# Layer 1's pooling mixer: the projection and the group maps folded into one matrix, token tiles, and pooling as products with integers

## The chip, the core and the metric

The kernel runs on one core of one Trainium2 chip. The metric is the device time of one execution in microseconds (us). TensorE (PE) multiplies, PEld loads its weights, VectorE (DVE) and ScalarE (ACT) work on tiles, GpSimd (POOL) does small tile work and indirect DMAs, SyncE (SP) issues most weight loads. The instruction streams of the engines are fixed when the program is built: each engine takes its instructions in order, and an instruction waits for the tiles that it reads.

## The reference, cut to what matters

1024 tokens of 1024 channels pass two layers. Layer 0 mixes by attention beside an mLSTM, layer 1 by pooling, and each ends in a mixture of 16 experts, each of which chooses its 128 tokens:

```python
def pool_mixer(h, w_in, w_grp, s_pool):
    u = h @ w_in
    S = cumsum(u) padded with one zero row
    for gi, w in enumerate((2, 4, 8, 16)):          # 256 channels each
        lo = w // 2; hi = w - 1 - lo
        a = clip(t - lo, 0, n - 1); e = clip(t + hi, 0, n - 1)
        outs.append((S[e + 1] - S[a]) / (e - a + 1) - u_group)
    y = einsum('bngc,gce->bnge', p, w_grp)
    return y * s_pool

x = x + m2 * pool_mixer(modulate(x, g_norm1, m0, m1), ...)
h = modulate(x, g_norm2, m3, m4)
x = x + m5 * ec_moe(h, w_router, w_gate, w_up, w_down)
```

`modulate` is an RMS norm, times (1 + scale), plus a shift. Pooling acts on tokens alone and the group map on channels alone, so the two can change places.

## The kernel before, in words

Products that need fp32 accuracy are made of three fast ones: `split` writes a high part with an ACT cast (L57) and the rest with a DVE subtraction (L58), and `mm3` (L51 to L53) multiplies high by high, low by high, and high by low.

Layer 0 ends in `out0`: per tile of 128 tokens the output projection `y` (512 wide), the new stream x, `half` (transposes L883, ACT copies L886, squares L888), `logits` (L894, 16 wide, plain fp32), `norm2`, `router`, and `normed`, which stores the normed tokens to G. Then comes `topk`, in which each expert finds its 128 tokens: 15 rounds, each three DVE comparisons (L978), one tiny PE product (L983) and a few DVE instructions on it, then two scans, a transpose (L1016) and a cast (L1018). After that `moe`: `choose` builds an expert's list with a one-hot of DVE (L1174) and eight products (L1178), `gather` fetches its rows with an indirect DMA of POOL (L1166), and the expert is three products of 1024x1024, g, u and d. SP streams the weights in 1 MB pieces through a ring of 17 slots (`cyc`). The last expert's rows go into the stream by products with one-hot matrices (`rows`, L1271 to L1279), so that no indirect DMA stands at the end.

Layer 1 works channel by channel. `w_normed` multiplies a group of `w_in_odd` (256 columns, 1 MB) by the scale (L1343) and sums it with the shift on POOL (L1340 to L1344); for the first group in the last expert of layer 0, for the other three in `layer1`. `turn` (L1292) transposes the stream tile by tile. `channels(i)` makes u of one group with 96 products of 512 columns (channels on the partitions, tokens along the row), and DVE walks along the tokens: times the rows' norms (L1434), doubling window sums (L1440), mean minus token (L1444), the edges (L1448, L1449), and the split. `mapped` multiplies by the group map, 256 wide, for `into_stream` (L1464), which runs for group i - 1 after the products of group i; `done_half` puts half of the logits between the products of the last group. The last group ends tile by tile (L1497) with the norm, the router and the store of the normed tokens. `topk` and `moe` of layer 1 follow, then the final norm.

In `topk` the code sets the order; between its instructions a list scheduler, at build time, places what is ready of the code around it. Which instructions of the changed code stand there is shown below.

Of the kernel before, what the change touches and what calls it, by code (L numbers as in the profile page):

```python
# [11 lines left out]
F32 = mybir.dt.float32  # L12
# [10 lines left out]
D = 1024  # L23
N = 1024
NCTX = 256
NT = 8
# [6 lines left out]
ORDER = (3, 2, 1, 0)  # L33
# [8 lines left out]
class Kern:  # L42
# [996 lines left out]
    def out0(self):  # L1039

        tc, nc, I = self.tc, self.nc, self.I
        with ExitStack() as es:
# [26 lines left out]
            xs = [resid(0), resid(1)]  # L1069
            self.norm2_load(0, (row("r_a2"), row("r_s2")), c.tile([128, KB + 1, 16], F32, name="wr"),  # L1070
# [37 lines left out]
            self.topk(tp, [(psl, "pl")])  # L1108


    def moe(self, l, last=False):
        tc, nc, I = self.tc, self.nc, self.I
        with ExitStack() as es:
# [93 lines left out]
            for e in range(16):  # L1207
# [21 lines left out]
                if e == 15 and not last:  # L1229
                    T = lambda nm, shape: self.topp.tile(shape, F32, name=nm)  # L1230
                    self.al, self.ones = T("al1", [128, 8]), T("ones1", [128, 1])
                    nc.gpsimd.memset(self.ones, 1.0)
# [5 lines left out]
                if e == 15 and not last:  # L1238
                    wn = self.w_normed(w0, self.R(9, (128, KB, 256), F32), xr3.tile([128, 4, 256], F32, name="X3"), nc.vector)
                if e == 15:  # L1240

                    xs, xp = [], []
                    for q, slot in enumerate(self.cyc[l][5:9]):
# [42 lines left out]
            if not last:  # L1286
                self.ss1 = self.topp.tile([128, NT], F32, name="ss1")
                self.xs, self.xp, self.W = xs, xp, [[self.quarters(wn[0])]]
                self.HH = [[self.R(i, (128, 4, 512)) for i in q] for q in ((6, 7), ("X1", "X2"))]
                self.HL = [[self.R(i, (128, 4, 512)) for i in q] for q in ((8, "X0"), (1, 2))]  # L1290

                def turn(t):  # L1292
                    b, os_ = t // 4, slice((t % 4) * 128, (t % 4 + 1) * 128)
                    for c in range(2):
                        ps = pst.tile([128, 4, 128], F32, name="tr", tag="tr")
                        for j in range(4):
                            nc.tensor.transpose(ps[:, j], xs[t][:, (4 * c + j) * 128:(4 * c + j + 1) * 128], self.idf)
                        self.turned = self.split(self.HH[b][c][:, :, os_], self.HL[b][c][:, :, os_], ps)

                for t in range(NT + 1):  # L1300
                    if t < NT:
                        rows(t)
                    if t:
                        turn(t - 1)
                for t in range(NT):
                    square(xs[t], self.ss1[:, t:t + 1])
                self.W[0].append(self.w_shift(wn[1]))
                return
# [19 lines left out]
    def w_raw(self, i):  # L1328

        raw, g = self.R(5, (128, KB, 256), F32), ORDER[i]  # L1330
        self.nc.sync.dma_start(raw, self.I["w_in_odd"][0].rearrange("(k p) n -> p k n", p=128)[:, :, g * 256:(g + 1) * 256])
        return raw

    def w_normed(self, raw, out, t, engine):

        G = self.nc.gpsimd
        acc, tmp = t[:, 0:2], t[:, 2:4]
        for q in range(4):
            b = slice(2 * q, 2 * q + 2)
            G.tensor_tensor(tmp if q else acc, raw[:, b], self.mcol[:, 0, b, None].to_broadcast([128, 2, 256]), op=ALU.mult)  # L1340
            if q:
                G.tensor_tensor(acc, acc, tmp, op=ALU.add)
        engine.tensor_tensor(out, raw, self.al[:, :, None].to_broadcast([128, KB, 256]), op=ALU.mult)  # L1343
        G.tensor_tensor(acc[:, 0], acc[:, 0], acc[:, 1], op=ALU.add)  # L1344
        return out, acc[:, 0]

    def w_shift(self, s1):

        sh = self.topp.tile([128, 2], F32, name="sh1", tag="sh1", bufs=2)
        ps = self.pst.tile([128, 512], F32, name="tr", tag="tr")  # L1350
        for m in range(2):
            self.nc.tensor.matmul(ps[:, m:m + 1], s1[:, m * 128:(m + 1) * 128], self.ones, start=True, stop=True)
        self.nc.vector.tensor_copy(sh, ps[:, 0:2])
        return sh

    def layer1(self):
        tc, nc, I = self.tc, self.nc, self.I
        LO = [w // 2 for w in (2, 4, 8, 16)]
        with ExitStack() as es:
            P = lambda name, bufs=1, **k: es.enter_context(tc.tile_pool(name=name, bufs=bufs, reuse_waits="tile", **k))  # L1360
            gp, hf, sp, c, pst = P("g1", 2), P("hf1", 2), P("st1", 2), P("c1"), self.pst
            up = tc.alloc_tile_pool(name="u1", bufs=1, reuse_waits="tile")
            psu, psy, psl = P("psu1", 2, space=PSUM), P("psy1", 1, space=PSUM), P("psl1", 1, space=PSUM)
            HH, HL, W, xs = self.HH, self.HL, self.W, self.xs

            rc = c.tile([128, 4, 16], F32, name="rc")
            for g, lo in enumerate(LO):
                for t in range(lo):
                    nc.gpsimd.memset(rc[:, g, t:t + 1], 1.0 / (t + lo))
                for t in range(lo - 1):  # L1370
                    nc.gpsimd.memset(rc[:, g, 8 + t:9 + t], 1.0 / (2 * lo - 1 - t))
            r8 = self.rstd(c, self.ss1, D, "r8", True)

            def more_w(i):
                t = self.R(10 if i == 1 else 0, (128, 4, 256), F32)
                raw = self.w_raw(i)
                raw, s1 = self.w_normed(raw, raw, t, nc.gpsimd)
                W.append((self.quarters(raw), s1))

            more_w(1)  # L1380

            ms = c.tile([128, 1024], F32, name="ms")
            with tc.issue_after(self.turned):
                nc.scalar.dma_start(ms, bc(self.MOD[8]))
                sr = up.tile([128, 1024], F32, name="sr", tag="pf")
                nc.scalar.dma_start(sr, bc(I["s_pool"][0]))
                nc.vector.tensor_tensor(ms, ms, sr, op=ALU.mult)

            def invariants():

                R = up.tile([128, 1024], F32, name="R1")
                for q in range(2):
                    ps = pst.tile([128, 512], F32, name="tr", tag="tr")
                    for t in range(4):
                        nc.tensor.matmul(ps[:, t * 128:(t + 1) * 128], r8[:, 4 * q + t:4 * q + t + 1].to_broadcast([128, 128]),
                                         self.idf, start=True, stop=True)
                    nc.scalar.copy(R[:, q * 512:(q + 1) * 512], ps)
                return R

            def channels(i, between=iter(())):  # L1400

                g, lo = ORDER[i], LO[ORDER[i]]
                w = 2 * lo
                cs = slice(g * 256, (g + 1) * 256)
                rg = hf.tile([128, 2, 256], F32, name="rg", tag="hf")
                nc.scalar.dma_start(rg, I["w_pool_grp"][0, g].rearrange("(k p) n -> p k n", p=128))
                nc.vector.tensor_tensor(rg, rg, ms[:, None, cs].to_broadcast([128, 2, 256]), op=ALU.mult)
                gh = gp.tile([128, 2, 256], F32R, name="gh", tag="gh")
                gl = gp.tile([128, 2, 256], F32R, name="gl", tag="gl")
                self.split(gh, gl, rg)  # L1410
                sh = self.w_shift(W[i][1]) if i else W[0][1]
                pu = [psu.tile([128, 1024], F32, name="u", tag="u") for m in range(2)]
                for q in range(2):
                    for m in range(2):
                        for k in range(KB):
                            a = slice(m * 128, (m + 1) * 128)
                            wh, wl = W[i][0][k // 4]
                            self.mm3(pu[m][:, q * 512:(q + 1) * 512], wh[:, k % 4, a], wl[:, k % 4, a], HH[q][k // 4][:, k % 4],
                                     HL[q][k // 4][:, k % 4], k == 0, k == KB - 1)
                        next(between, None)  # L1420
                if i == 0:
                    self.R1 = invariants()
                if i < 3:
# [53 lines left out]
            for i in range(1, 4):  # L1477
                if i + 1 < 4:
                    more_w(i + 1)
# [131 lines left out]
```

## Time and profile before

| | |
|---|---|
| median of 3 runs | 2328.53 us (2322.75 to 2331.19) |
| profiled execution | 2325.28 us, of which the span of the profile is 2323.5 us |
| TensorE busy | 2133.2 us (92%) |
| VectorE busy | 1974.5 us (85%) |
| ScalarE, GpSimd busy | 1407.9 us (61%), 258.1 us (11%) |
| mean granted clock of TensorE | 0.959 |

The span is that of one profiled execution. A share near 100% means that the engine works nearly all the time, but the shares are means over stages with different limits: layer 0 up to about 850 us, its choice up to 889 us, its experts up to about 1481 us, layer 1's mixer and choice up to about 1712 us, and its experts to the end.

### The profile page before, as it was taken

The page shows a single profiled execution, that of the slowest core. Times are in us where ns is not written, and L with a number is a line of the kernel's source. Part 1 is how long each engine was busy: PE and PEld are TensorE (multiplying, and loading weights), DVE is VectorE, ACT ScalarE, POOL GpSimd, SP SyncE. Part 2 cuts the span into 40 slices and gives each one's busy share as a digit, 9 for nine tenths or more (in the row PEclk, how much of TensorE's full clock was granted, in tenths as well). Part 3 has the DMA queues.
Part 4 walks back from the last instruction along what each step waited for, and adds up shares of the span by engine and source line. Part 5 has one row for each costly group of instructions (what it writes and reads, how often), then busy time and mean ns, then how long its engine had stood idle before and what let it go on. Part 6 is the DMA issues. An engine that isn't in the chain of part 4 may idle for free.

```text
span 2323.5 us, 29647 instructions
## 1 busy us (share of the span) xinstructions
PE 2133.2 (92%) x10339; PEld 1702.9 (73%) x10339; DVE 1974.5 (85%) x3043; ACT 1407.9 (61%) x1994; POOL 258.1 (11%) x369
## 2 busy tenths in 40 slices
PE   6889999998988966999999999889749999999997
PEld 3768887776666854888888887568637888888875
DVE  7888755999997558999999998885789999999986
ACT  6412224777784224777777777622337777777774
POOL 0111110000000010000000010550300000000001
PEclk9989999999999987999999999999769999999999
DMA  7566653243325466999999995323859999999974
GB/s 275 201 234 231 244 197 111 75 115 99 90 83 182 163 259 244 365 380 388 385 378 392 380 379 204 111 63 118 326 193 355 387 386 381 388 384 379 391 247 154
DMA packets 206634, 599.39 MB, mean 258 GB/s; under 512 B 16708, under 2 KB 60180, under 8 KB 205460
## 3 DMA queue, kind: packets, MB, share of 16 engines
q1 hardware_dynamic: 168480, 481.81, 55.0%
q0 software_dynamic: 20704, 74.49, 11.1%
q10 hardware_dynamic: 17300, 41.20, 4.8%
q8 instruction: 81, 1.33, 0.2%
q14 instruction: 69, 0.57, 0.1%
HBM read 544.87 MB, written 52.58 MB: 257 GB/s over the span
## 4 chain that ended last, share of the span: by engine, by line
PE 56%; DVE 8%; issue 2%; ACT 2%; POOL 1%; DMA 1%; ACTq 0%; POOLq 0%; DVEq 0%; SPq 0%
PE u L51 6%; PE u L52 6%; PE u L53 6%; PE g L53 5%; PE g L52 5%; PE g L51 5%; PE d L52 5%; PE d L53 5%; PE d L51 5%; PE tr L1158 2%; DVE wl L58 2%; PE y L51 2%; PE y L53 2%; PE y L52 1%; DVE tjunk L978 1%
## 5 line engine op out<-in xcount | busy, mean ns | idle before, releaser
L58 DVE TENSOR_TENSOR wl<-R,wh 128x1024 fp32r<-128x1024 f32 x512 | 614.5, 1236 | 39.0 <-ACT wh L57 36.5
L57 ACT CAST wh<-R 128x1024 fp32r<-128x1024 f32 x512 | 534.1, 1052 | 172.9 <-PE d L53 56.6
L58 DVE TENSOR_TENSOR wl<-X,wh 128x1024 fp32r<-128x1024 f32 x178 | 211.0, 1220 | 13.9 <-ACT wh L57 13.1
L57 ACT CAST wh<-X 128x1024 fp32r<-128x1024 f32 x178 | 186.0, 1050 | 54.8 <-PE d L53 23.2
L52 PE MATMUL d<-wl,ah 128*128 128x512 f32 x512 | 203.6, 398 | 5.5 <-DVE wl L58 5.5
L51 PE MATMUL d<-wh,ah 128*128 128x512 f32 x512 | 205.2, 401 | 2.9 <-DVE o L1193 2.9
L51 PE MATMUL g<-wh,xh 128*128 128x512 f32 x512 | 205.8, 402 | 1.5 <-ACT xh L57 1.5
L52 PE MATMUL g<-wl,xh 128*128 128x512 f32 x512 | 203.2, 397 | 1.8 <-DVE wl L58 1.8
L51 PE MATMUL u<-wh,xh 128*128 128x512 f32 x512 | 204.4, 399 | 0.0
L52 PE MATMUL u<-wl,xh 128*128 128x512 f32 x512 | 202.6, 396 | 0.6 <-DVE wl L58 0.6
L53 PE MATMUL g<-wh,xl 128*128 128x512 f32 x512 | 203.2, 397 | 0.0
L53 PE MATMUL d<-wh,al 128*128 128x512 f32 x512 | 202.7, 396 | 0.0
L53 PE MATMUL u<-wh,xl 128*128 128x512 f32 x512 | 202.1, 395 | 0.0
L57 ACT CAST wh<-raw 128x1024 fp32r<-128x1024 f32 (+1 forms) x112 | 115.5, 1037 | 57.1 <-PE pp L53 15.3
L58 DVE TENSOR_TENSOR wl<-raw,wh 128x1024 fp32r<-128x1024 f32 (+1 forms) x112 | 131.6, 1202 | 13.1 <-ACT wh L57 12.3
L693 ACT ACTIVATE e<-se 128x512 f32<-128x512 f32 x160 | 93.4, 596 | 42.9 <-PE se L691 30.5
L52 PEld LDWEIGHTS d<-wl,ah 128*128 128x128 f32 x512 | 96.9, 189 | 30.2 <-DVE wl L58 9.3
L51 PEld LDWEIGHTS d<-wh,ah 128*128 128x128 f32 x512 | 96.8, 189 | 25.1 <-ACT ah L57 3.8
L51 PEld LDWEIGHTS g<-wh,xh 128*128 128x128 f32 x512 | 97.2, 190 | 23.7 <-ACT xh L57 2.5
L52 PEld LDWEIGHTS g<-wl,xh 128*128 128x128 f32 x512 | 97.1, 190 | 23.7 <-DVE wl L58 2.6
L52 PEld LDWEIGHTS u<-wl,xh 128*128 128x128 f32 x512 | 96.4, 188 | 23.2 <-DVE wl L58 1.9
L53 PEld LDWEIGHTS d<-wh,al 128*128 128x128 f32 x512 | 96.8, 189 | 22.6 <-DVE al L58 0.5
(561 smaller groups left out, 4833.1 us busy)
## 6 DMA issues: line engine op xcount, KB each, us to landing
R<-in_w_exp_gate SPq DMA_DIRECT2D x87, 1024.0 KB
R<-in_w_exp_down SPq DMA_DIRECT2D x85, 1024.0 KB
R<-in_w_exp_up SPq DMA_DIRECT2D x79, 1024.0 KB
wm<-in_w_mod POOLq DMA_DIRECT2D x80, 512.0 KB, 5.2
X<-in_w_exp_up SPq DMA_DIRECT2D x33, 1024.0 KB
X<-in_w_exp_down SPq DMA_DIRECT2D x30, 1024.0 KB
X<-in_w_exp_gate SPq DMA_DIRECT2D x26, 1024.0 KB
raw<-in_w_exp_up SPq DMA_DIRECT2D x16, 1024.0 KB
```

Source lines behind the costliest of these rows:

```text
L51: mm(ps, lh, rh, start=start, stop=False)
L52: mm(ps, lh, rl, start=False, stop=False)
L53: self.mark = mm(ps, ll, rh, start=False, stop=stop).ins
L57: self.nc.scalar.copy(hi, src)
L58: return self.nc.vector.tensor_tensor(lo, src, hi.bitcast(F32), op=ALU.subtract).ins
L693: nc.scalar.activation(e, ps, AF.Exp)
L978: V.tensor_scalar(junk[:, j], A, thr[:, j:j + 1].bitcast(F32), None, op0=ALU.is_ge, op1=ALU.add, accum_out=cnt[:, j:j + 1])
L1158: nc.tensor.transpose(ps[:, j * 128:(j + 1) * 128], src[:, (4 * q + j) * 128:(4 * q + j + 1) * 128], self.idf)
```

## The change

One matrix stands for the projection and the group maps. WD holds, for each group g of 256 columns, `w_in_odd` of that group times (`w_pool_grp[g]` times m2 times `s_pool`, divided by the window w). It is made in layer 0's choice: `fold` transposes each group of `w_in_odd` (64 transposes of 128x128, L1144), multiplies in plain fp32 (64 products 256 wide, L1158), copies the results out with ACT (16 copies of the transposes, L1146, and 16 of the products, L1160, all 512 wide), and ACT's queue stores WD to DRAM, 1 MB a group. The loads are `w_pool_grp` (1 MB) and `w_in_odd` (4 MB), of which three groups go on POOL's queue.

In the last expert of layer 0, WD is loaded (4 pieces of 1 MB, SP) and split into high and low. `w_normed`, `w_shift`, `turn` and the squares are gone from there.

Layer 1 goes by tiles of 128 tokens. `prep(t)` norms the rows (ACT square, POOL root, DVE scaling), transposes them and applies scale and shift on the way out of PSUM (eight ACT instructions of 128x128), then splits. `project(t)` makes z = h WD, 48 products of 512 columns, and splits z into two row tiles. `pooled(t)` multiplies z by integer matrices over the tokens: for each group, high and low by a 128x128 band of integers, and once by a tile with the eight neighbouring rows on each side (`halo`, written by small POOL DMAs from the tiles beside it). It adds the result to the stream and calls `half`; `finish(t)` does logits, norm, router and store. `pooled` runs two tiles behind `project`. The slot lists `cyc` and the tiles that hold the stream change.

```diff
+            fold = self.fold_load()
...
             self.topk(tp, [(psl, "pl")])
+            self.fold(fold, psy)
...
+        for g in range(4):
+            nxt = turned(g + 1) if g < 3 else None
+            out = self.R(3 + g % 2, (128, KB, 256), F32)
+            for k in range(0, KB, 2):
+                ps = psp.tile([128, 2, 256], F32, name="y", tag="y")
+                for i in range(2):
+                    for m in range(2):
+                        nc.tensor.matmul(ps[:, i], wt[:, m, (k + i) * 128:(k + i + 1) * 128], rg[:, g, m],
+                                         start=m == 0, stop=m == 1)
+                nc.scalar.copy(out[:, k:k + 2], ps)
+            nc.scalar.dma_start(self.WD.rearrange("(k p) n -> p k n", p=128)[:, :, g * 256:(g + 1) * 256], out)
+            wt = nxt
...
-                    w0 = self.w_raw(0)
...
+                    for i, slot in enumerate(self.cyc[0][9:13]):
+                        w = self.R(slot, (128, 4, 512))
+                        nc.sync.dma_start(w.bitcast(F32), wd[i // 2, i % 2])
+                        WL.append(w)
...
-                    wn = self.w_normed(w0, self.R(9, (128, KB, 256), F32), xr3.tile([128, 4, 256], F32, name="X3"), nc.vector)
...
+                for w, slot in zip(WL, self.cyc[0][13:16] + self.cyc[0][0:1]):
+                    h = self.R(slot, (128, 4, 512))
+                    for q in (0, 2):
+                        self.split(h[:, q:q + 2], w[:, q:q + 2], w[:, q:q + 2].bitcast(F32))
+                    self.W1.append((h, w))
...
+                    for k in range(KB):
+                        wh, wl = W[2 * q + k // 4]
+                        self.mm3(ps, T[:, 0, k], T[:, 1, k], wh[:, k % 4], wl[:, k % 4], k == 0, k == KB - 1)
+                    cs = slice(q * 512, (q + 1) * 512)
+                    self.split(zh[:, cs], zl[:, cs], ps)
...
+                        nc.gpsimd.dma_start(halo[(t - 1) % 3][16 + 8 * i:24 + 8 * i], z[0:8])
...
+                        for n, (m, z) in enumerate(((4 * kind + g, Z[t][0]), (4 * kind + g, Z[t][1]),
+                                                    (12 + g, halo[t % 3]))):
+                            nc.tensor.matmul(ps[:, i], pc[:, m], z[:, gs], start=n == 0, stop=n == 2)
...
+            ready = [prep(0), prep(1)]
...
+            for t in range(NT):
+                z = project(t, ready[t])
+                next(z)
...
+                y = pooled(t - 2) if t >= 2 else iter(())
+                for _ in y:
+                    pass
+                for _ in z:
+                    pass
+                if t + 2 < NT:
+                    ready.append(prep(t + 2))
+                if t >= 2:
+                    finish(t - 2)
```

How this moves instructions on the engines shows at three places. The first is TensorE's stream at the end of layer 0's choice; before, it reads (L1016 turns the chosen ranks, L1178 makes expert 0's list):

```order
L1004 LDWEIGHTS low
L1004 MATMUL pl<-cc,low 128x2
L1005 LDWEIGHTS blk
L1005 MATMUL pl<-cc,blk 128x1
L1016 MATMUL pl<-idf,pg 128x128
L1178 LDWEIGHTS oh
L1178 MATMUL tr<-tk,oh 128x5
```

In the changed kernel, where `choose`'s product has line 1232, the same place reads (R_7600 is the scaled group maps, R_8888 and R_8939 the transposed groups 2 and 3):

```order
L1004 LDWEIGHTS low
L1004 MATMUL pl<-cc,low 128x2
L1005 LDWEIGHTS blk
L1005 MATMUL pl<-cc,blk 128x1
L1158 MATMUL y<-R_7600,R_8888 128x256
L1016 MATMUL pl<-idf,pg 128x128
L1158 MATMUL y<-R_7600,R_8888 128x256 x11
L1158 MATMUL y<-R_7600,R_8939 128x256 x16
L1232 LDWEIGHTS oh
L1232 MATMUL tr<-tk,oh 128x5
```

Between the transpose L1016 and the list of expert 0 there stand 27 products of the fold, 11 of group 2 and 16 of group 3. Ahead of these, the rounds (L983) have 37 more products and 48 of the 64 transposes between them, one to twelve in a gap; the other 16 transposes are ahead of the rounds.

The second place is VectorE's stream at the end of layer 0's last expert; before, it reads (wl is a weight's low part, o the expert's output, L1275 adds its rows to the stream):

```order
L58 TENSOR_TENSOR wl<-R_13658,wh 128x1024 x2
L58 TENSOR_TENSOR wl<-R_13660,wh 128x1024 x2
L58 TENSOR_TENSOR wl<-R_13662,wh 128x1024 x2
L1343 TENSOR_TENSOR R_13919<-R_13833,al_13829 128x2048
L1193 SCALAR_TENSOR_TENSOR o<-d,cg,m_8827 128x1024
L58 TENSOR_TENSOR wl<-R_13919,wh 128x1024 x2
L58 TENSOR_TENSOR ofl<-o,ofh 128x1024
L1275 TENSOR_TENSOR raw_13930<-raw_13930,g 128x1024
```

In the changed kernel, X and R_14060 are WD's pieces, and L1331 adds the rows:

```order
L58 TENSOR_TENSOR wl<-raw_13885,wh 128x1024 x2
L58 TENSOR_TENSOR X_14054<-X_14054,R_14267 128x1024 x2
L1247 SCALAR_TENSOR_TENSOR o<-d,cg,m_9050 128x1024
L58 TENSOR_TENSOR X_14056<-X_14056,R_14272 128x1024 x2
L58 TENSOR_TENSOR ofl<-o,ofh 128x1024
L58 TENSOR_TENSOR X_14058<-X_14058,R_14277 128x1024 x2
L872 SCALAR_TENSOR_TENSOR a2c<-n2col,g_103 128x8
L58 TENSOR_TENSOR R_14060<-R_14060,R_14282 128x1024 x2
L1331 TENSOR_TENSOR R_14146<-R_14146,g 128x1024
L1331 TENSOR_TENSOR R_14149<-R_14149,d 128x1024
```

The product with the scale, L1343, and with it POOL's eight L1340 to L1344 of the same weights are gone; eight subtractions for WD have come, two ahead of o and six between o and the first row addition.

The third place is TensorE's stream in layer 1. Before, a group's 96 products of u end and the group maps of the group before begin (X and R are the turned tokens, gh and gl a group map):

```order
L52 MATMUL u<-R_14067,wh 128x512
L53 MATMUL u<-X_14063,wl 128x512
L51 MATMUL y<-gh,R_14458 128x256
L52 MATMUL y<-gl,R_14458 128x256
L53 MATMUL y<-gh,R_14459 128x256
```

In the changed kernel the same place in a tile's work reads (z of tile t, then y of tile t - 2, raw the integers, ha the halo):

```order
L52 MATMUL z<-X_14056,R_14635 128x512
L53 MATMUL z<-R_14272,R_14635 128x512
L1445 MATMUL y<-wh,raw_14376 128x256
L1445 MATMUL y<-wl,raw_14376 128x256
L1445 MATMUL y<-ha_14381,raw_14376 128x256
```

A tile has 48 products of z, and the 12 pooling products of the tile two behind stand after the first 24 of them.

## Rows read from the trace of the kernel before

**Rows 1.** Busy time of the engines; TensorE's clock in 40 slices
```profile
PE 2133.2 (92%) x10339; PEld 1702.9 (73%) x10339; DVE 1974.5 (85%) x3043; ACT 1407.9 (61%) x1994; POOL 258.1 (11%) x369
...
PEclk9989999999999987999999999999769999999999
```

**Rows 2.** Windows: busy us (instructions) by engine, granted clock, DMA share, GB/s
```profile
950.00:1400.00 450.00, 450.00 (x2124) 365.81 (x2123) 430.45 (x429) 353.40 (x367) 33.15 (x25) 1.00 1.02 383
...
1460.00:1470.00 10.00, 6.46 (x20) 4.58 (x21) 10.00 (x7) 4.07 (x5) 9.05 (x6) 0.83 0.55 114
...
1660.00:1670.00 10.00, 9.49 (x47) 9.39 (x45) 7.96 (x22) 3.69 (x12) 4.23 (x7) 0.50 1.02 409
```

**Rows 3.** The chain of waits, 1480 to 1710: start, us, what
```profile
1486.37 1.23 DVE raw L1275
...
1502.53 1.28 ACT L120
...
1508.31 7.28 DMA R<-in_w_in_odd
...
1525.80 4.02 POOL R L1343
...
1619.85 0.80 PE pl L894 x8
```

**Rows 4.** The timeline of VectorE: start, us, engine, line, operation
```profile
1661.91 0.42 DVE L1497 TENSOR_TENSOR R<-R,u 128x256 f32<-128x256 f32 x1 [1.01 <-PE u L53]
...
1675.79 0.29 DVE L964 COPY A<-pl 128x128 f32<-128x128 f32 x1 [0.57 <-PE pl L962]
```

**Rows 5.** Timeline of TensorE and GpSimd in layer 0's choice, idle before
```profile
873.90 0.17 PE L983 MATMUL pl<-cnt,blk 128*128 128x3 bf16 x1 [1.57 <-DVE tjunk L978]
...
886.00 0.47 PE L1016 MATMUL pl<-idf,pg 128*128 128x128 f32 x1 [1.80 <-DVE pg L1014]
...
888.19 0.38 PE L1178 MATMUL tr<-tk,oh 128*128 128x5 bf16 x8 [1.72 <-DVE oh L1174]
...
889.25 1.99 POOL L1166 DMA_INDIRECT xg<-G,ci  x1 [27.25 <-DVE ci L1182]
```

**Rows 6.** Timeline of TensorE at the end, plain fp32 products
```profile
2303.50 1.02 PE L1271 MATMUL g<-X,idf 128*128 128x512 f32 x2
...
2303.95 0.80 PE L1272 MATMUL g<-ofh,to 128*128 128x512 f32 x1
...
2304.59 0.39 PE L1273 MATMUL g<-ofl,to 128*128 128x512 f32 x1
```

**Rows 7.** The timeline of TensorE in the first expert
```profile
899.40 0.39 PE L51 MATMUL g<-wh,xh 128*128 128x512 f32 x1
...
908.92 0.40 PE L53 MATMUL g<-wh,xl 128*128 128x512 f32 x1
```

**Rows 8.** The timeline of TensorE, eight transposes before the first expert
```profile
894.49 1.97 PE L1158 MATMUL tr<-idf,xg 128*128 128x128 f32 x8 [5.92 <-DMA xg<-G,ci]
```

**Rows 9.** ScalarE's groups by line, 1480 to 1510: busy us, mean ns, idle
```profile
L1284 ACT ACTIVATE jf<-R 128x1024 bf16<-128x1024 f32 x4 | 4.3, 1078 | 0.0
```

**Rows 10.** Timeline of VectorE and GpSimd, layer 0's last expert
```profile
1454.85 2.43 DVE L58 TENSOR_TENSOR wl<-R,wh 128x1024 fp32r<-128x1024 f32 x2
...
1461.55 16.19 DVE L58 TENSOR_TENSOR wl<-R,wh 128x1024 fp32r<-128x1024 f32 x7
...
1479.87 1.27 DVE L1193 SCALAR_TENSOR_TENSOR o<-d,cg,m 128x1024 f32<-128x1024 f32 x1
...
1475.07 1.59 POOL L1344 TENSOR_TENSOR X<-X 128x256 f32<-128x256 f32 x1
```

**Rows 11.** The timeline of TensorE, 256-wide products of the group maps
```profile
1595.54 0.28 PE L53 MATMUL y<-gh,R 128*128 128x256 f32 x1
...
1595.66 0.28 PE L51 MATMUL y<-gh,R 128*128 128x256 f32 x1
```

**Rows 12.** DMA issues: KB each, us from issue to landing
```profile
wm<-in_w_mod POOLq DMA_DIRECT2D x80, 512.0 KB, 5.2
```

More of the change, by code (lines that the diff above doesn't have):

```diff
@@ new lines, in odd_columns, with fold, turned @@
+    def odd_columns(self, g, slot, queue):
+        raw = self.R(slot, (128, KB, 256), F32)
+        queue.dma_start(raw, self.I["w_in_odd"][0].rearrange("(k p) n -> p k n", p=128)[:, :, g * 256:(g + 1) * 256])
+        return raw
+    def fold(self, loaded, psp):
+        nc = self.nc
+        rg, raw = loaded
+        raws = [raw] + [self.odd_columns(g, slot, nc.gpsimd) for g, slot in ((1, 7), (2, 8))]
+        def turned(g):
+            wt = self.R(5 + g % 2, (128, 2, 1024), F32)
+            for m in range(2):
+                for q in range(2):
+                    ps = psp.tile([128, 512], F32, name="y", tag="y")
+                    for j in range(4):
+                        nc.tensor.transpose(ps[:, j * 128:(j + 1) * 128], raws[g][:, 4 * q + j, m * 128:(m + 1) * 128],
+                                            self.idf)
+                    nc.scalar.copy(wt[:, m, q * 512:(q + 1) * 512], ps)
+            return wt
+        wt = turned(0)
+        raws.append(self.odd_columns(3, 9, nc.gpsimd))
+        for g in range(4):
[4 more added lines that the diff above has]
+                for i in range(2):
+                    for m in range(2):
+                        nc.tensor.matmul(ps[:, i], wt[:, m, (k + i) * 128:(k + i + 1) * 128], rg[:, g, m],
[3 more added lines that the diff above has]
+            wt = nxt
@@ L1286, in moe @@
             if not last:
[L1287 to L1304, printed above, removed]
+                self.xs, self.xp, self.W1 = xs, xp, []
+                for w, slot in zip(WL, self.cyc[0][13:16] + self.cyc[0][0:1]):
[3 more added lines that the diff above has]
+                    self.W1.append((h, w))
                 for t in range(NT):
-                    square(xs[t], self.ss1[:, t:t + 1])
-                self.W[0].append(self.w_shift(wn[1]))
+                    rows(t)
                 return
@@ L1380, in layer1 @@
[L1380 to L1391, printed above, removed]
-                for q in range(2):
[L1393 to L1398, printed above, removed]
@@ L1507, in layer1 @@
+            for t in (NT - 2, NT - 1):
+                for _ in pooled(t):
+                    pass
+                finish(t)
             self.topk(tp, [(psl, "pl"), (pst, "tr")])
@@ L1593, in rope_table, with pool_tables @@
                           1).astype(np.float32)
+def pool_tables():
+    t = np.arange(128)
+    m = np.zeros((128, 16, 128), np.float32)
+    edge = np.ones((128, 2, 4), np.float32)
+    for g, w in enumerate(POOLS):
+        lo, hi = w // 2, w - 1 - w // 2
+        inside = (t[:, None] >= t - lo) & (t[:, None] <= t + hi)
+        counts = np.minimum(t + lo, w), np.full(128, w), np.minimum(128 - t + lo, w)
+        for kind, n in enumerate(counts):
+            m[:, 4 * kind + g] = inside - np.diag(n)
+        edge[:, 0, g], edge[:, 1, g] = w / counts[0], w / counts[2]
+        r = np.arange(8)[:, None]
+        m[0:8, 12 + g] = m[8:16, 12 + g] = r - 8 >= t - lo
+        m[16:24, 12 + g] = m[24:32, 12 + g] = r + 128 <= t + hi
+    return m, edge
 def kernel(x, c, ctx, c_ctx, w_mod, b_mod, g_norm1, g_norm2, w_in_even, w_out_even, g_qnorm, g_knorm, w_conv, b_gate,
```

235 lines of the change are left out of this document (92 added, 143 removed).

## The prediction

> **What bounds the kernel now.** I read the page first, then stretches of time. TensorE is busy 92% of the span and VectorE 85% [rows 1], but the stages differ, and the reader should see three kinds. In the experts TensorE has no gap at full clock, and DMA runs at its ceiling too (share 1.02) [rows 2]; nothing of this change touches that. In layer 0's choice TensorE does next to nothing: in each of 15 rounds it waits 1.57 us for VectorE and works 0.17 [rows 5]. This is room, but room at a low clock and on the path: whatever stands in TensorE's stream ahead of L983 or of expert 0's list delays the first expert. The third kind is the change over to layer 1 and its mixer. From the end of the last o, 1479.87 + 1.27 = 1481.14 [rows 10], to the copy A at 1675.79 with which the choice begins [rows 4], 194.65 us pass. In them TensorE has 384 products of u. In the first expert 42 such products (the two rows of [rows 7] are the first and the last) start within 9.52 us, so 0.232 us each at full clock, and u needs 89.2 us. With maps, transposes and logits about 146 us of work stand there; some 49 us are waits. The chain of waits names them: a load of `w_in_odd` 7.28, POOL's products on it (one of 4.02 at their end) [rows 3], and VectorE's walks over the windows.
>
> **The change, part by part.**
>
> *The fold in the choice.* A plain fp32 product of 512 columns is not one pass: from the start of L1271 to the start of L1273 are 1.09 us [rows 6], in which one L1271 (two records) and one fast product L1272 stand; less 0.23, L1271 takes 0.86, so a 256-wide one 0.43 at full clock and, by the ratio of the two clocks, 0.86 at half. A transpose took 1.97 / 8 = 0.25 us at the low clock [rows 8].
>
> Behind L1016 stand 27 of these products. Before, the list's products start 1.7 us after L1016's end (886.47 to 888.19) [rows 5], while VectorE casts and builds the one-hot; that covers 1.7 of 27 x 0.43 = 11.6, and 9.9 are on the path, since the gather (889.25 [rows 5]) and the first expert wait for the list. I take 10.
>
> The other 37 products and 48 transposes stand in 15 gaps. They are 37 x 0.43 + 48 x 0.25 = 27.9 us of work for 15 x 1.57 = 23.6 us of room, so 4.3 if spread evenly; four products in a gap exceed it by 0.15, twelve transposes by 1.4, and single ones at half clock by 1.9. I take 5. The first round stands behind two transposes of a group that POOL's queue loads into a slot which is free only when `y` ends, while SP's loads fill the DMA: 0 to 4, I take 1. Two ACT copies come between the last tile's router steps: a 1024-wide ACT instruction takes 1.08 [rows 9], half of it 0.55 each, of which I count 0.6 in all. The fold costs 10 + 5 + 1 + 0.6, about 17. From below: were a product no dearer than a fast one, 27 x 0.23 - 1.7 = 4.5, with nothing in the rounds. From above, all at half clock: 27 x 0.86 - 1.7 = 21.5, and 37 x 0.86 + 12 - 23.6 = 20, with 1.6 about 43. I stay near full clock because TensorE has no gap once the products follow one another, and in the first expert it is at full pace within three or four us of such work.
>
> The clock is the weak place. In 1660 to 1670 TensorE was busy 9.49 of 10 us, with transposes, 16-wide logits and a few maps, and its granted clock stayed at 0.50, the level of 1.2 GHz [rows 2]. The Trainium skill, "TensorE: Matmul & The Clock Gate", Part 4 (PE-mode transpose), says that a transpose does not count as busy work for the clock in the way that a product does; the trace agrees with it in that window, and by it the 64 transposes would run at 0.25 us, as I have charged them, but the plain products between them might not reach full clock either, which is the first rival below.
>
> The stores of WD (4 MB, ACT's queue) hold two ring slots, so two of the first 17 weight pieces come late; a piece is a twelfth of an expert, and the two are used more than an expert after the start, so I charge nothing. If that cover fails, each us of lateness costs one.
>
> *The end of layer 0's last expert.* There VectorE's seven subtractions take 16.19 us, 2.31 each, while POOL multiplies; two just before take 2.43, 1.22 each [rows 10]. With POOL's work gone the seven take 8.5, L1343 goes, and two subtractions for WD come (2.4): VectorE is at o by 1461.55 + 10.9 = 1472.5 instead of 1479.87. The product d needs 48 x 0.232 = 11.1 us of TensorE after about 1462, and has only 6.46 of 10 us in 1460 to 1470 [rows 2]; so o moves to about 1474. I take -6, between 0 (something else holds d) and -7.4.
>
> The Trainium skill, "SBUF — State Buffer", section "Who interferes with whom", says that a VectorE instruction with two SBUF inputs and a GpSimd instruction that reads SBUF exclude each other; the rows agree (2.31 against 1.22).
>
> *Layer 1, its start.* After o, VectorE has six subtractions for WD and one for o (7 x 1.22 = 8.5) and six row additions of 1.23 [rows 3], so 15.9. ACT then has a copy, the table load 1.28 [rows 3] and two squares (1.08 each and their read-outs), about 5, and behind these the load of the router's weights, on which 16 small products wait that stand ahead of some of the transposes: 2.5, below the 5.2 of a 512 KB load [rows 12]. Transposes, ACT's shifts and the split of the first tile: about 6. z starts 30 us after o (22 to 36), with 2 us lost to the low clock.
>
> *Layer 1, its stream.* 384 products of z, 89.2. Pooling: 72 products for six tiles, 0.12 each (the starts of [rows 11]), 8.6. Transposes: 48 for z and 48 for `half`, at half of 0.25, 11.8. Logits of six tiles: 96 records at 0.80 / 8 [rows 3], 9.6. Sum 119.2. VectorE has about 9 us a tile (two 1024-wide norm instructions, one scaling and some ten half rows, each about half of 1.22) and ACT about as much; both are under TensorE's 14.5, so I call the stream TensorE's. The halo of tile t - 2 needs the last rows of z(t - 1); 24 products of z (5.6) and some transposes cover it.
>
> *Its end.* After z(7): split 1.3, a halo DMA of 8 rows about 3, 24 pooling products at half clock 5.8, then squares, logits and router. Before, 13.9 us pass from the last addition (1661.91) to A (1675.79) [rows 4], with three older tiles' norms on VectorE in them. I take 16 for all, between 11 and 23.
>
> 30 + 2 + 119.2 + 16 = 167 against 194.65: -27. Layer 1's choice and experts stay: the ring's slots come free from z(7) on, far ahead of the first gather.
>
> *Sum.* 17 - 6 - 27 = -16 on the profiled execution's 2325.28: 2309.3. The median of the runs is 3.25 above that execution, so 2312.5, say 2313. Ranges of the terms (10 to 25, 0 to -7, -20 to -33) give 2300 to 2324 for this case.
>
> **Rivals.** *The fold stays at half clock*, as 1660 to 1670 did: 43 instead of 17, so 2339, at the edge of slower by 0.5%. For it: the choice's granted work is short bursts between waits, with 64 transposes. Against it: 27 dense products at the end.
>
> *The halo is late*, and the kernel slower. Each tile's z(t) stands behind y(t - 2) in TensorE's order, and y reads rows that go by DMA from POOL, four of them a tile, one after another. The cover is about 7 us from the end of z(t - 1); less 1.3 for the split, the DMA must land within 5.5. The nearest row is 5.2, for 512 KB [rows 12]. Each us beyond is paid seven times; at 9.6 us it costs 28 and the time is 2341. It decides above 9.6. For it: nothing but the narrow margin; against it: 8 rows are 32 KB.
>
> *Layer 1 gains little.* The 384 products are unchanged, so only the waits can go; if the start costs 36, the low clock holds for transposes and logits, and a tile waits for its preparation, -12 instead of -27: 2328, no change.
>
> *The fold is hidden*, its products at 4.5: about 2301.
>
> **How the numbers follow.** Forecast 0.58, half clock 0.12, halo late 0.06, little gain 0.12, fold hidden 0.12. About 0.5% (11.6 us) is what a measurement of this kernel tells from no change, so faster is below 2316.9. Most of the forecast's range (0.49 of 0.58) and the hidden fold lie there: 0.61. The rest of it, little gain and half of the half-clock case: 0.27. The other half and the late halo: 0.12. The range takes the hidden fold's 2301 with the low ends of the other terms, 2294, to just under the half-clock case, 2337.
>
> **What would show it.** Right: the gather of expert 0 some 17 us later than 889, with 27 products L1158 ahead of the list, at 0.43; subtractions of 1.22 in the last expert; from o to A about 167 us, with z at 0.232 and no wait of y on ha. Wrong: L1158 at 0.86 or a granted clock of 0.5 through the choice; L1445 waiting for a DMA in each tile; z starting later than 36 us after o.

## The result, and the profile after

The changed kernel takes 2314.97 us (median of 6 runs, 2307.66 to 2317.55), the kernel before 2325.81 in the same comparison: a ratio of 0.9946, with a 95% interval of 0.9925 to 0.9968. That is 10.8 us less, for a forecast of 2313. The sum was right by luck: one large term was too hopeful (layer 1), two costs had not been charged (late rows, and the front of layer 0's end), and what made up for them is a gain of some 22 us in the experts that has nothing to do with the folding. The profiled execution after takes 2315.16 us, its span is 2313.3.

The page's first part answers to [rows 1]. TensorE's total is no smaller (2135.7 us against 2133.2), and VectorE's has fallen by 67 us, which shows how little such sums tell.

```profile
PE 2135.7 (92%) x10387; PEld 1715.2 (74%) x10387; DVE 1907.6 (82%) x2982; ACT 1432.7 (62%) x2068; POOL 222.7 (10%) x341
```

Stages tell more. Each boundary below is an instruction's start or end in the two traces, in us from the span's start.

| from, to | before | after | difference |
|---|---|---|---|
| start, first product of `out0` | 736.3 | 743.8 | +7.5 |
| `out0`, to its last product | 111.9 | 119.2 | +7.3 |
| to the copy A of layer 0's choice | 7.7 | 7.0 | -0.7 |
| A, gather of expert 0 | 33.3 | 48.2 | +14.9 |
| gather, first product of expert 0 | 7.1 | 12.2 | +5.1 |
| to the end of the last o | 584.8 | 567.7 | -17.1 |
| to A of layer 1 (mixer) | 194.7 | 178.5 | -16.2 |
| A, gather of layer 1's expert 0 | 36.8 | 33.3 | -3.5 |
| to the last o | 583.9 | 573.8 | -10.1 |
| to the end | 27.0 | 29.6 | +2.6 |

These make -10.2. First the fold. TensorE's stream at the end of the choice, after, answers to [rows 5]; the number at a row's end is the idle time before it and what ended it:

```profile
874.10 0.66 PE L1144 MATMUL y<-idf,R 128*128 128x128 f32 x2 [4.09 <-DMA R<-in_w_in_odd]
874.55 0.21 PE L983 MATMUL pl<-cnt,blk 128*128 128x3 bf16 x1
...
896.68 1.97 PE L1158 MATMUL y<-R,R 128*128 128x256 f32 x8
898.49 0.17 PE L983 MATMUL pl<-cnt,blk 128*128 128x3 bf16 x1
...
905.44 0.33 PE L1016 MATMUL pl<-idf,pg 128*128 128x128 f32 x1 [1.27 <-DVE pg L1014]
905.61 11.82 PE L1158 MATMUL y<-R,R 128*128 128x256 f32 x54
917.26 0.34 PE L1232 MATMUL tr<-tk,oh 128*128 128x5 bf16 x8
...
928.67 1.94 PE L1212 MATMUL tr<-idf,xg 128*128 128x128 f32 x8 [11.07 <-DMA xg<-G,ci]
930.44 0.79 PE L51 MATMUL g<-wh,xh 128*128 128x512 f32 x1
```

A plain fp32 product leaves two records, so 54 of them are the 27 products, in 11.82 us: 0.44 each, as priced. The list follows L1016 by 11.82 instead of 2.19 us. The wait for `w_in_odd` ahead of the first round is there too, 4.09 long. What the prediction had not got is the last wait: the gathered rows land 11.07 us after TensorE has finished the list, against 5.92 in [rows 8]. Why they come later was not tried.

The windows answer to [rows 2] (busy us of each engine, granted clock, DMA share, GB/s):

```profile
870.00:890.00 20.00, 14.18 (x73) 11.91 (x73) 12.92 (x85) 6.05 (x11) 8.27 (x8) 0.74 0.77 281
890.00:910.00 20.00, 17.16 (x91) 13.75 (x90) 14.62 (x91) 6.92 (x13) 0.00 (x0) 1.00 0.92 358
910.00:930.00 20.00, 8.93 (x50) 7.90 (x49) 2.82 (x5) 5.46 (x8) 1.92 (x1) 0.80 0.87 308
...
1540.00:1640.00 100.00, 100.00 (x539) 81.14 (x538) 45.78 (x83) 44.65 (x109) 24.14 (x50) 1.00 0.26 84
1650.00:1660.00 10.00, 2.54 (x16) 2.36 (x16) 1.45 (x6) 0.40 (x2) 1.12 (x2) 0.62 1.03 414
```

The later part of the fold, and with it the 27 products, ran at a granted clock of 1.00 (2.4 GHz); in 870 to 890 it was 0.74. In layer 1 TensorE has no gap for 100 us, so no tile waits for its halo there. Only behind the last z does the halo show. This is TensorE there, the end that answers to [rows 4]:

```profile
1648.52 0.39 PE L53 MATMUL z<-R,R 128*128 128x512 f32 x1
...
1650.89 0.28 PE L1445 MATMUL y<-wl,raw 128*128 128x256 f32 x1
1658.63 0.55 PE L1445 MATMUL y<-ha,raw 128*128 128x256 f32 x1 [7.46 <-DMA ha<-wl]
```

In the last expert, VectorE's subtractions answer to [rows 10]: 1.2 us each where they were 2.31 beside POOL's work, so the four below take 4.63. The Trainium skill, "SBUF — State Buffer", section "Who interferes with whom", says that a VectorE instruction with two SBUF inputs contends with a GpSimd instruction that reads SBUF. With GpSimd's work gone the trace agrees.

```profile
1489.32 4.63 DVE L58 TENSOR_TENSOR wl<-raw,wh 128x1024 fp32r<-128x1024 f32 x4
1493.86 2.35 DVE L58 TENSOR_TENSOR X<-X,R 128x1024 fp32r<-128x1024 f32 x2
1496.82 1.28 DVE L1247 SCALAR_TENSOR_TENSOR o<-d,cg,m 128x1024 f32<-128x1024 f32 x1 [0.60 <-PE d L53]
```

Last, the surprise. Both traces have a full TensorE in the experts, at full clock, and yet the products follow one another faster after (start, duration):

```profile
1478.11 0.39 PE L52 MATMUL d<-wl,ah 128*128 128x512 f32 x1
...
1483.10 0.39 PE L53 MATMUL d<-wh,al 128*128 128x512 f32 x1
```

These are 22 steps in 4.99 us, 0.2268 each; before, [rows 7] give 0.232. A layer's experts have 16 x 3 x 48 = 2304 products, and the mean steps over 1000 to 1400 (steps above 0.26 us, at waits and other instructions, left out) are 0.2325 before and 0.2271 after: 12.4 us a layer. This mean is called the pace below. No line of the diff touches these products; only the order of the ring's slots and the places of the tiles changed.

### The profile page after: what moved, and what is told of

The parts are those of the page before. It is cut to its first block, busy times and chain, and to the rows that moved or that the text cites. A ratio compares the mean times of both kernels' runs of the same rounds, so it can differ in the third digit from the quotient of the medians.

```text
span 2313.3 us, 29775 instructions
## 1 busy us (share of the span) xinstructions
PE 2135.7 (92%) x10387; PEld 1715.2 (74%) x10387; DVE 1907.6 (82%) x2982; ACT 1432.7 (62%) x2068; POOL 222.7 (10%) x341
## 4 chain that ended last, share of the span: by engine, by line
PE 75%; DMA 7%; DVE 7%; issue 6%; ACT 3%; POOL 1%; ACTq 0%; POOLq 0%; DVEq 0%; SPq 0%
PE g L52 5%; PE g L53 5%; PE u L51 5%; PE g L51 5%; PE u L52 5%; PE u L53 5%; PE d L52 5%; PE d L53 5%; PE d L51 5%; DMA wm<-in_w_mod 3%; PE tr L1212 2%; PE pp L52 2%; PE pp L53 2%; PE pp L51 2%; DMA R<-in_w_exp_gate 1%
## 5 line engine op out<-in xcount | busy, mean ns | idle before, releaser
L58 DVE TENSOR_TENSOR wl<-R,wh 128x1024 fp32r<-128x1024 f32 x496 | 585.1, 1220 | 19.6 <-ACT wh L57 6.6
L57 ACT CAST wh<-R 128x1024 fp32r<-128x1024 f32 x496 | 519.2, 1055 | 127.8 <-PE g L53 43.5
L51 PE MATMUL g<-wh,xh 128*128 128x512 f32 x512 | 203.1, 397 | 1.5 <-ACT xh L57 1.5
L51 PE MATMUL d<-wh,ah 128*128 128x512 f32 x512 | 201.7, 394 | 2.9 <-DVE o L1247 2.9
L52 PE MATMUL g<-wl,xh 128*128 128x512 f32 x512 | 200.7, 392 | 1.9 <-DVE wl L58 1.9
L51 PE MATMUL u<-wh,xh 128*128 128x512 f32 x512 | 202.2, 395 | 0.0
L52 PE MATMUL d<-wl,ah 128*128 128x512 f32 x512 | 200.2, 391 | 1.9 <-DVE wl L58 1.9
L52 PE MATMUL u<-wl,xh 128*128 128x512 f32 x512 | 200.0, 391 | 1.1 <-DVE wl L58 1.1
L53 PE MATMUL g<-wh,xl 128*128 128x512 f32 x512 | 200.5, 392 | 0.0
L53 PE MATMUL u<-wh,xl 128*128 128x512 f32 x512 | 199.8, 390 | 0.0
L53 PE MATMUL d<-wh,al 128*128 128x512 f32 x512 | 199.7, 390 | 0.0
L52 PEld LDWEIGHTS g<-wl,xh 128*128 128x128 f32 x512 | 96.8, 189 | 22.2 <-DVE wl L58 3.3
L52 PEld LDWEIGHTS d<-wl,ah 128*128 128x128 f32 x512 | 96.2, 188 | 23.0 <-DVE wl L58 3.9
L51 PEld LDWEIGHTS d<-wh,ah 128*128 128x128 f32 x512 | 96.2, 188 | 22.6 <-ACT ah L57 3.7
L51 PEld LDWEIGHTS g<-wh,xh 128*128 128x128 f32 x512 | 96.8, 189 | 21.4 <-ACT xh L57 2.4
L52 PEld LDWEIGHTS u<-wl,xh 128*128 128x128 f32 x512 | 96.2, 188 | 22.0 <-DVE wl L58 2.8
L53 PEld LDWEIGHTS g<-wh,xl 128*128 128x128 f32 x512 | 96.5, 188 | 19.9
```

Of the source, the lines that this page charges most:

```text
L51: mm(ps, lh, rh, start=start, stop=False)
L52: mm(ps, lh, rl, start=False, stop=False)
L53: self.mark = mm(ps, ll, rh, start=False, stop=stop).ins
L57: self.nc.scalar.copy(hi, src)
L58: return self.nc.vector.tensor_tensor(lo, src, hi.bitcast(F32), op=ALU.subtract).ins
```

## Why the experts run faster: addresses

Theory: the fast pace comes from where the experts' tiles lie in SBUF. The change drops three small tiles (`ones1`, `ss1`, `sh1`) from the pool `topk`, and so what is allocated behind them moves by 128 bytes. Rival: it is of the execution or of the chip. e1_before is the kernel before, unchanged.

> The kernel before, profiled once more. In the experts the changed kernel's products start 0.2271 us apart (mean, 1000 to 2200), those of the kernel before 0.2325, though the code of the experts differs only in the order of the ring's slots. Theory 'placement': the pace belongs to the program (where its tiles lie), so it is 0.2325 again and the time about 2325. Rival 'execution': the pace belongs to the execution or the chip, and it may come out at 0.227, with a time near 2300.

It took 2324.37 us (one run), its products 0.2325 apart. The rival fell. e2_shift128 gives the changed kernel one pad of 128 bytes, ahead of the slots X and of the experts' tiles, so that both lie where they lay before:

```diff
+            self.shift = self.topp.tile([128, 32], F32, name="shift")
+            nc.gpsimd.memset(self.shift, 0.0)
```

> The changed kernel with a tile of 128 bytes a partition added ahead of the four X slots and the expert tiles, which puts them at the addresses that they have in the kernel before (X0 at 160640 instead of 160512). Theory 'addresses': the experts' pace goes from 0.227 back to 0.2325, 2304 products a layer, so about 12 us a layer slower, 2335 to 2340. Rival 'slot order' (or execution): the pace stays at 0.227 and the time at 2315.

2337.24 us, a ratio to before of 1.0045 (1.0032 to 1.0058), pace 0.2325 in both layers. So the order of the slots, which is still the changed one, is not the cause either. e6_shift_expert_tiles has its pad of 128 bytes behind the slots X instead, so these stay where the change put them.

```diff
+            shift = c.tile([128, 32], F32, name="shift")
+            nc.gpsimd.memset(shift, 0.0)
```

> The changed kernel with 128 bytes a partition added behind the X slots, so that only the tiles of the experts (xh, xl, ah, al and the small ones) lie where they lie in the kernel before; the X slots stay. Theory 'stationary tiles': their address sets the pace, it is 0.2325 and the time about 2338. Rival 'X slots': the address that the weights are loaded to sets it, the pace stays at 0.227 and the time at 2315.

2340.11 us (one run), pace 0.2325: it is the experts' own tiles, xh, xl, ah and al among them, and not the slots. The other way round, b_shift128 is the kernel before with the pad of e2_shift128.

> The kernel before with 128 bytes a partition added ahead of the X slots and the expert tiles (X0 at 160768, xh at 204224, which is 256 more than in the changed kernel). Theory 'addresses modulo 256': the experts' pace becomes 0.227 and the kernel before, with nothing else changed, gains about 2 x 12 us: 2302. Rival 'these very addresses, or a larger period': the pace stays at 0.2325 and the time at 2326.

2305.22 us, 0.9918 (0.9898 to 0.9938) of the kernel before, pace 0.2271. So 128 unused bytes are worth more than the whole change. It ran again beside a later experiment:

> The kernel before with 128 B of pad, again, on the same chip as the others of this call: 2303 to 2308, so that what the change is worth at an equal pace of the experts is read within one call. If addresses are the cause, products 0.2271 apart; if the earlier gain was of one chip, 0.2324 and 2320 to 2330.

2303.26 us, 0.9904 (0.9886 to 0.9921), with a pace of 0.2271; this stretch has 10 steps in 2.27 us:

```profile
1202.10 0.39 PE L52 MATMUL g<-wl,xh 128*128 128x512 f32 x1
...
1204.37 0.39 PE L53 MATMUL g<-wh,xl 128*128 128x512 f32 x1
```

b_shift64 pads by 64 bytes.

> The kernel before with 64 B of pad instead of 128, the experts' tiles at an address that leaves 128 modulo 256 (before leaves 64, the 128 B version 192). Theory one (only 64 modulo 256 is bad): pace 0.2271, 2303 to 2308. Theory two (the start must leave 192 modulo 256 for the fast pace): 0.2324, 2322 to 2328. Something between the two paces would say that the tiles' several addresses count one by one.

2315.01 us, one run: between the two, as its third case said. The mean steps differ by the kind of product: 0.2313 from L51 to L52, 0.2268 from L52 to L53, 0.2292 from L53 to L51, 0.2291 in the mean. The built programs place xh at these byte offsets; xl, ah and al lie at the same remainder:

```
kernel                 offset of xh   modulo 256   step, us
before                 204096          64          0.2325
before + 64 B          204160         128          0.2291
before + 128 B         204224         192          0.2271
changed                203968         192          0.2271
changed, moved back    204096          64          0.2325
```

That the offset sets the pace is shown. By which rule (which tiles, what remainder) is not: three remainders are few, the experts' tiles moved all together in each of these kernels, and the slots X stayed in e6_shift_expert_tiles alone.

## The front: work that waits for loads

Two stages ahead of the choice lost 14.8 us. VectorE in `out0`, after: the product of the fold's two scale rows (L1120) stands in its stream and waits 5.83 us for the load of `s_pool`, and behind it, and behind four scalings of the group maps (L1122), stands `wr` (L873), for which TensorE waits.

```profile
760.18 1.23 DVE L1120 TENSOR_TENSOR R<-R 128x1024 f32<-128x1024 f32 x1 [5.83 <-DMA R<-in_s_pool]
761.33 1.22 DVE L58 TENSOR_TENSOR wl<-ro,wh 128x1024 fp32r<-128x1024 f32 x1
762.46 2.49 DVE L1122 SCALAR_TENSOR_TENSOR R<-R,R 128x512 f32<-128x512 f32 x4
764.87 1.22 DVE L58 TENSOR_TENSOR wl<-ro,wh 128x1024 fp32r<-128x1024 f32 x1
766.00 0.28 DVE L873 TENSOR_TENSOR wr<-wr,a2c 128x128 f32<-128x128 f32 x1
```

```profile
766.43 1.86 PE L894 MATMUL pl<-wr,xT 128*128 128x16 f32 x8 [5.35 <-DVE wr L873]
```

e3_compute_late calls `fold_load` with the third tile, behind a row addition of `out0`; e3b_all_late holds its loads, too, behind the load of x for the fifth tile.

```diff
-            fold = self.fold_load()
...
+                self.lastx = nc.scalar.dma_start(x, I["x"][0, t * 128:(t + 1) * 128]).ins
...
+                if t == 2:
+                    with tc.issue_after(last), tc.issue_after(self.lastx):
+                        fold = self.fold_load()
```

> The changed kernel with fold_load called in the third tile of out0, its VectorE part held behind the second tile's row addition; its loads stay where they were in ScalarE's order. Theory 'the product with s_pool held VectorE': from the first y product to the last, 119 us becomes 112, and the time falls by 7, to about 2308. Rival 'out0 is late for another reason' (the loads, DMA traffic): no change, 2315.

> As the run before it, with the loads of w_pool_grp, of the two rows and of the first group of w_in_odd held as well, behind the load of the fourth x tile on ScalarE's queue. Theory 'the early load and the order around it cost attention 7.5 us': the first y product moves from 743.8 back to about 736, the time falls by another 7, to about 2300. Rival: the loads are now late for the choice, the fold's first transposes wait, and what is gained is lost there: 2308.

2306.65 us (0.9914, 0.9895 to 0.9932 of before) and 2299.48 us (0.9871, 0.9847 to 0.9895). In e3b `out0` takes 111.5 us from 737.7 on, about as before (111.9 from 736.3). That VectorE's wait made `out0` late is shown by e3. What the held loads add in e3b is not: the profiled executions of the two differ by 1.2 us only (2303.50 and 2302.33), and no trace here shows where the 7 us between the medians lie. With the front clear, the stage from A to the gather is 48.8 us in e3b, so the choice pays 15.5 whatever happens ahead of it. In e3b the list stands behind the products as it did:

```profile
892.46 11.82 PE L1160 MATMUL y<-R,R 128*128 128x256 f32 x54
904.11 0.34 PE L1234 MATMUL tr<-tk,oh 128*128 128x5 bf16 x8
```

The gain at the very start is less sure: the first product of `out0` starts at 743.8 to 746.3 in the three kernels with the change's order, and at 729.5 to 740 in all others, the kernel before with its pads among them, so single executions differ there by some us. In e3 two of the fold's loads, `w_pool_grp` and the first of `w_in_odd`, are still issued early, at 689.58 and 701.44, and it starts at 739.3; so these two alone do not make the late start, and its cause stays open.

## The list behind the products

e8_rest_behind (on top of e4_hold, below, which takes 2299.73) moves the last group's 16 products behind expert 0's list.

```diff
+            for g in range(3):
+                nxt = turned(g + 1)
+                multiplied(g, wt, lambda k: psp.tile([128, 2, 256], F32, name="y", tag="y"))
...
+                with tc.issue_after(self.listed):
+                    self.fold_rest(lambda k: halves[k // 4][:, k // 2 % 2])
```

> The run e4_hold with the 16 products of the fold's last group moved behind expert 0's list, into the time in which its gather runs. Theory 'products ahead of the list delay the first expert one for one': 16 x 0.43 = 6.9 us less ahead of the list, of which about 6 are hidden by the gather: 6 us under e4_hold, about 2288. Rival 'the first expert waits for weights or for the gather anyway': the gather is issued 6.9 earlier but the first product of g is not; no change.

A miss: 2308.38 us (0.9931, 0.9911 to 0.995). From A the gather leaves after 41.3 us instead of 49.4, and its rows are waited for 5.55 instead of 11.26 us. But eight of the products now stand between these rows and the expert itself, the first four at 0.9 each (3.62 for eight records), with a granted clock of 0.59 in 905 to 912. And the last store of WD, which frees ring slots, leaves at 913.09 instead of 901.01. Expert 1's rows are late next:

```profile
905.22 1.94 PE L1218 MATMUL tr<-idf,xg 128*128 128x128 f32 x8 [5.55 <-DMA xg<-G,ci]
906.95 3.62 PE L1157 MATMUL u<-R,R 128*128 128x256 f32 x8
910.37 2.06 PE L1157 MATMUL d<-R,R 128*128 128x256 f32 x8
...
923.17 1.54 PE L1218 MATMUL tr<-idf,xg 128*128 128x128 f32 x6 [5.28 <-DMA xg<-G,ci]
```

SP's queue shows the stall. It holds three pieces for 19.53 us; that is no loss of this order, for in e4_hold the like is 18.33 (the last line). But in the 20.8 us behind that hold it issues three pieces, where e4_hold issues seven.

```profile
886.78 19.53 SPq L1188 DMA_DIRECT2D R<-in_w_exp_up  x3
...
913.97 0.37 SPq L1188 DMA_DIRECT2D R<-in_w_exp_down  x1
927.16 0.37 SPq L1188 DMA_DIRECT2D R<-in_w_exp_up  x1
```

```profile
884.30 18.33 SPq L1184 DMA_DIRECT2D R<-in_w_exp_up  x3
```

From its first product to its result, expert 0 takes 71.2 us, against 63.3 in e4_hold.

The work that left the list held up the expert instead.

## The last halo

The four halo writes of 32 KB issued at 1600 to 1606, with DMA nearly idle (23 GB/s), landed after 2.2 us; the last two went out at 1650.04 and 1651.97, among weight loads at a DMA share of 1.03, and took 5.6 and 6.4. This is the view of DMA issues for each of the two stretches (KB, us to landing):

```profile
ha<-wh POOLq DMA_DIRECT2D x2, 32.0 KB, 2.2
ha<-wl POOLq DMA_DIRECT2D x2, 32.0 KB, 2.2
```

```profile
ha<-wh POOLq DMA_DIRECT2D x1, 32.0 KB, 5.6
ha<-wl POOLq DMA_DIRECT2D x1, 32.0 KB, 6.4
```

Earlier writes beside a load took 4.5 to 5.2 us (1584.95 to 1586.57) and 4.9 to 6.6 (1618.33 to 1620.98); but those of 1636.45 to 1637.46 landed in 2.5 to 2.9 although the DMA share was 1.04 and 0.92 in the two us from 1636 on. TensorE had other work then and waited for none of them. Theory: the last two wait behind layer 1's weights. e4_hold (on e3b) holds the first weight slot, e9_hold_all the first twelve, by a tiny GpSimd copy that reads the landed halo:

```diff
+            for slot in self.cyc[1][:12]:
+                hold = self.R(slot, (128, 2, 1024), F32)
+                nc.gpsimd.tensor_copy(hold[0:32, 0, 0:8], halo[(NT - 2) % 3][0:32, 0:8].bitcast(F32))
```

> The run e3b_all_late with the first weight slot of layer 1's experts written by one tiny GpSimd copy that reads the last halo tile, so that the weight loads begin only when those rows have landed. Theory 'the last halo waits behind the weights': in the changed kernel y of tile 6 waits 7.5 us for rows of 8 KB while the DMA share is 1.03; held back, the wait falls to 2 or 3 and the choice begins about 5 us earlier after z(7): 2294 against e3b's 2299.5. Rival 'a small DMA from GpSimd takes that long anyway': no gain, and the late weights cost: 2300 or more.

> e3b's order of the fold, and in layer 1 the first twelve weight pieces of its experts are held (a copy of 8 columns by GpSimd writes each of their slots after the halo of tile 6 has landed), so that no weight piece travels with that halo; before, only one slot was held and seven pieces left at 1622 to 1634. Theory (the halo waits behind the bulk weight loads): DMA share of 1630 to 1642 falls well below 1, the halo lands 2 to 4 us after its last issue instead of 6.3, the idle time of y on it falls from 7.1 to 2 to 4, and the time to 2294 to 2298, since the first expert needs 8 MB only some 50 us later. Rival (the wait is the halo's own way: z's split, GpSimd's two issues, the landing of small rows): y waits 6 to 7.5 as before and the time stays at 2298 to 2302, or above it if the weight pieces are then late.

Both missed. e4: 2299.73 us, y still idle for 7.11; from 1617 on, seven pieces of other slots had left before. e9: 2304.12 us (0.9909, 0.9894 to 0.9924), still 6.50, and layer 1's experts some 3 us longer than in e3b, since the held loads come later. DMA was not empty even there: a store of normed tokens (1629.01) and a piece of a slot that was not held (1630.75) fill it until 1636, and the halo lands behind them.

```profile
1634.00:1636.00 2.00, 0.00 (x0) 0.00 (x0) 0.00 (x0) 0.00 (x0) 0.00 (x0) 0.50 1.00 385
1636.00:1638.00 2.00, 0.00 (x0) 0.02 (x1) 0.00 (x0) 0.00 (x0) 0.00 (x0) 0.50 0.12 43
```

```profile
1638.01 0.55 PE L1447 MATMUL y<-ha,raw 128*128 128x256 f32 x1 [6.50 <-DMA ha<-wl]
```

So queueing behind bulk traffic fits most of these rows, and is not proven by taking the traffic away. What the wait costs was measured by itself: e10_no_last_halo is e3b without the two last writes. It leaves them out of the computation (tile 6 pools over zeros or older rows at its end), so it prices the wait and is no version to keep.

```diff
-                if t:
+                if 0 < t < NT - 1:
```

> e3b's order of the fold, and the first rows of the last tile's z are not handed to tile 6, so its last few rows pool over zeros or older rows: left out of the computation to price the last halo in whole. Theory (the halo's way stands on the path that sets the choice of layer 1): y of tile 6 waits for nothing after z(7), and the choice begins 5 to 7 us earlier, 2293 to 2296. Rival (the norms and the router of tiles 5 and 6, on VectorE and GpSimd, stand right behind it): the choice begins 0 to 3 us earlier and the time is 2297 to 2301.

2292.43 us (0.986, 0.9835 to 0.9885): 7.1 less than e3b, whose interval against before (0.9847 to 0.9895) overlaps this one; the stage tells more, the mixer is 168.6 us against 176.6. TensorE goes through tile 6 without a stop, and at 0.28 a product, not 0.41:

```profile
1635.76 0.28 PE L1447 MATMUL y<-ha,raw 128*128 128x256 f32 x1
1635.87 0.28 PE L1447 MATMUL y<-wh,raw 128*128 128x256 f32 x1
```

The norms behind, the rival of that run, were not the limit.

## Why the prediction was right in its number, and where not

- *The fold in the choice*, +17: +14.9 (15.5 in e3b). The list cost 9.6 for 10. The rounds and the wait ahead of them share the rest: 30.9 us from the first round to L1016 for 28.8, so 2.1 for 5, and about 3 for 1. Right.
- *The half clock* came only at the start of the rounds. In 872 to 880 the granted clock was 0.50, and the eight transposes at 877.71 took 1.94 us, 0.24 each; the first products of the fold start at 879.44, and the clock was 0.76 in 880 to 882 and 1.00 from there on. The Trainium skill, "TensorE: Matmul & The Clock Gate", Part 4 (PE-mode transpose), says that a transpose does not count as busy work for the clock in the way that a product does; the trace does not speak against it, but 4 us of waiting stand there too, and no run here separates the two. The hidden fold did not come either.
- *Costs that were not charged*: the gathered rows land 5.1 us later, and the stages ahead of the choice take 14.8 us more, of which e3b took back most; 7.3 of these are VectorE's wait in `out0`, the other 7.5 are the less sure late start. The step that failed is that only the instructions in the choice, and the list, were charged; what `fold_load` puts ahead of and into `out0`, loads, scalings and the ACT work beside them, was given no price.
- *The last expert*, -6: first product to last o is 4.9 less in e2_shift128 (579.9) than before (584.8) at the same pace, and 5.3 less after than in b_shift128 (573.0). The last expert itself, from the o before it to its own, gave 7.4 (13.3 us for 20.7), the upper end of what was priced; 2 were lost again in the experts before it (491.6 from the first o to the last but one, for 489.3 in b_shift128), why was not tried. Right.
- *Layer 1*, -27: -16.2. The start took 28.5 for 30 (o's end 1498.10, z at 1526.60), the stream 122.1 for 121.2 with the clock's 2 us. The end took 27.9 for 16, above its bound of 23. That is the mis-sized term, and in it the halo. From the last z to the issue of the last write there were 3.2 us where the split was priced at 1.3, since its low part stands on VectorE behind a router step of an older tile; and the landing took 6.4 for about 3. Behind it comes time at the low clock. Without the halo, in e10, the end takes 17.5, against 25.8 in e3b. The late halo as a rival was thus wrong for each tile, and right for the last.
- *Rest, 0*: the experts' pace gave 12 and 10 us, and nothing in the prediction foresaw it: that the sum came out is luck. Without it the change is slower (e2_shift128, +11 us), which a reader of the number alone would not see. Layer 1's choice was 3.5 shorter and the end 2.6 longer; why was not tried.

At one pace the account is: fold and gather +20, experts' end -5, mixer -16, front +15, which makes +14 where e2_shift128 measures +11; e3b's order takes most of the +15 away. e3b (2299.48) stands beside before with its pad (2305.22 and 2303.26), measured at different times: 4 to 6 us, less than the half per cent that a measurement tells. The best full version that ran is e3b.

## What to carry to other kernels

A stage that nobody changed is checked too: when its time moves, compare the starts of its neighbouring instructions, since a full busy share shows no pace. Compare a change with a padded kernel before, or part of what is measured is the allocation. Work placed in idle time is charged with its loads, from where they are issued, and a small transfer that the end of a stage waits for is priced under the traffic that runs at that moment.

## What was not expected of the hardware

The step of back-to-back products of 512 columns changes from 0.2325 to 0.2271 us, 2.3%, by the offset of the experts' tiles, of which three remainders modulo 256 bytes were tried, at a granted clock of 1.00 in each case. And a write of 32 KB landed in 2.2 us with DMA nearly idle and in up to 6.6 with loads of 1 MB beside it; that these loads are the cause is not shown.
